# Two transformer blocks on one core: the last output projection by seven block products

## Chip, core and metric

One core of one Trainium2 chip. The metric is the device time of one execution in microseconds (us). Engines by their short names: PE is TensorE (PEld its weight loads), ACT ScalarE, DVE VectorE, POOL GpSimd, SP SyncE, whose queue issues every DMA of this kernel.

## The reference, cut to what matters

The last of three layers over T = 1024 tokens of width D = 1024 is banded attention with a gate:

```
q, z = split(h @ w_in, 2)                 # h: (1024, 1024)
out  = attention(q * HEAD_DIM**-0.5, k, v)  # 16 heads of 64, window 128, with sinks
y    = out * silu(z)                      # (1024, 1024)
h    = h + rms_norm_2(y @ w_out, post_g)  # the last projection, and the result
```

The layer before it has a projection of the same form, `y @ w_out` with y (1024, 2048). It is called the middle projection here. All arrays are fp32.

## The kernel before

Every large product is made from fp32 operands that are split in two fp32r parts, `hi` (an ACT copy) and `lo` (a DVE subtraction). `a @ b` becomes three matmuls: hi·hi, hi·lo, lo·hi. Weights come in pieces (`wraw`, 128x2x512 for projections), are split by `w_split_half` (L285 and L286: ACT makes `whi`, DVE makes `wlo`), and are fetched and split some pieces ahead, one half piece at a tick; a tick comes every four matmuls. At ticks the lanes advance too (generators that emit the work beside the matmuls), as do stores that were put off for some ticks and `jit`, which splits streamed activations. The program order on each engine is the order in which Python emits it, and each engine, SP's queue too, runs its own instructions in that order.

**Attention stage (`phase4`).** For each pair of heads p = 0 to 7 it computes q, the attention, and z. When a z half (512 tokens) is done, `make_z` takes its tanh on ACT and `gate_z` makes the gated output in two DVE operations (L2498, L2499); then ACT and DVE split it at once into `yb` hi and lo (L2501, L2503), which stay in SBUF: 16 halves of 128x512.

**Last projection (`run` in `out_proj`, L1884).** Two halves of 512 tokens (`half`), each by two halves of 512 output columns (`c`), each by four token tiles `j` of 128 and K = 8 slices of 128. That is 2 x 2 x 4 x 8 x 3 = 384 matmuls of 128x512. After each tile's last matmul ACT squares PSUM with a row sum (L1891) and DVE multiplies by the gain (L1892). For the first half `norm` finishes the tiles in a lane. For the second half the columns 512 to 1023 go tile by tile, and `last` finishes each tile: a sum, eleven more DVE operations on one column (an inverse square root by Newton steps, L456 to L470), two DVE operations of 128x512 that scale and add the residual (L1932), two stores.

**Middle projection (`run7`, L2044).** Its y and its weights are cut in four blocks each, and seven products of sums and differences of blocks replace eight. A product n = 0 to 6 is 512 tokens by 512 columns: four token tiles, each with its own PSUM bank. The weight differences (`TW`) were made by POOL during an earlier stage (`out_weights`) and kept in DRAM; the y blocks and their sums were stored to DRAM (`Y7`) and come back through `stream`, are split there by L1751 (ACT) and L1752 (DVE), about one product ahead of use. After the last matmuls of a product `evac` combines its PSUM tile with earlier products: an ACT copy (n = 0, 1), or a DVE sum (`plus`, L1998); finished output quarters go through `out`: an ACT square with row sum (L1993) and a multiplication by the gain (L1994, on POOL or DVE). After product 5, POOL adds the last quarter `c5` (L2015), and `last4` sends it through `out`.

`norm(0)` is the first token half's finish. It is emitted after product 4, beside product 5.

## Time and profile before

| what | value |
|---|---|
| median of 3 runs | 2471.33 us (2465.6 to 2472.78) |
| profiled execution | 2464.92 us, span 2463.1 us, granted PE clock 0.991 |
| busy in the span | PE 2407.2 us (98%), DVE 1451.9 (59%), ACT 1033.3 (42%), POOL 793.4 (32%) |

The times in rows count from the span's start. Matmuls are pipelined: a 128x512 matmul has a row of 389 ns while one follows the other every 227 ns (48 in 10.88 us). An engine's idle time stands in brackets behind the instruction that ended it, with what released it.

### The profile page before, as it was taken

What the parts mean: (1) busy time and instruction counts of PE and PEld (TensorE: products, weight loads), DVE (VectorE), ACT (ScalarE), POOL (GpSimd) and SP (SyncE); (2) the same over time, 40 slices, a digit from 0 to 9 for tenths busy, and PEclk for the clock granted to TensorE, in tenths of its full rate; (3) what the DMA queues carried; (4) which work ended last, traced back from release to release, by engine and by line L of the source; (5) the groups of instructions that cost most, each with busy time, mean ns of one, the idle gap of its engine ahead of it and who ended that gap; (6) DMA issues with size and microseconds to landing.
All of it is one profiled execution on the core that took longest, in us unless ns stands there. A gap on an engine that the chain in (4) does not pass through costs nothing.

```text
span 2463.1 us, 40015 instructions
## 1 busy us (share of the span) xinstructions
PE 2407.2 (98%) x14891; PEld 1899.8 (77%) x14891; DVE 1451.9 (59%) x3295; ACT 1033.3 (42%) x2539; POOL 793.4 (32%) x1023
## 2 busy tenths in 40 slices
PE   8999999999999999999999999999999998999998
PEld 6888777777777777777788777888878876777777
DVE  6765345545454345566747438656667587566545
ACT  4443222323232255664235223544545454566642
POOL 3443054433535032422420044545553033300000
PEclk8999999999999999999999999999999999999999
DMA  4334321111213355665834223334336842200033
GB/s 141 105 108 131 70 74 40 57 48 42 58 44 82 98 165 194 221 204 166 267 135 165 90 80 104 106 116 123 93 111 234 312 154 66 75 27 27 27 127 130
DMA packets 286262, 284.22 MB, mean 115 GB/s; under 512 B 27787, under 2 KB 208075, under 8 KB 286068
## 3 DMA queue, kind: packets, MB, share of 16 engines
q1 hardware_dynamic: 286068, 281.67, 36.6%
q8 instruction: 117, 1.92, 0.3%
q14 instruction: 77, 0.63, 0.1%
HBM read 206.87 MB, written 74.74 MB: 114 GB/s over the span
## 4 chain that ended last, share of the span: by engine, by line
PE 84%; DVE 6%; DMA 4%; ACT 3%; issue 2%; SPq 0%; POOL 0%; DVEq 0%; ACTq 0%; POOLq 0%
PE pd L349 39%; PE pd L391 8%; PE psP L391 8%; PE pb L2044 4%; PE pb L1884 4%; PE pd L1884 3%; PE psO L1157 2%; PE pb L1056 2%; PE pb L1122 2%; DMA vg<-Vd 1%; PE pb L349 1%; PE pd L2044 1%; DVE wlo L286 1%; PE pb L2338 1%; PE pb L743 1%
## 5 line engine op out<-in xcount | busy, mean ns | idle before, releaser
L349 PE MATMUL pd<-Ahi,wlo 128*128 128x512 f32 x1232 | 497.0, 403 | 5.0 <-DVE wlo L286 5.0
L349 PE MATMUL pd<-Ahi,whi 128*128 128x512 f32 x1232 | 496.6, 403 | 3.7 <-ACT Ahi L502 2.3
L349 PE MATMUL pd<-Alo,whi 128*128 128x512 f32 x1232 | 496.3, 403 | 1.7 <-DVE Alo L503 1.7
L286 DVE TENSOR_TENSOR wlo<-wraw,whi 128x512 fp32r<-128x512 f32 x348 | 278.7, 832 | 143.2 <-ACT whi L285 142.5
L349 PEld LDWEIGHTS pd<-Ahi,whi 128*128 128x128 f32 x1232 | 233.7, 190 | 56.5 <-ACT Ahi L502 3.1
L349 PEld LDWEIGHTS pd<-Alo,whi 128*128 128x128 f32 x1232 | 233.7, 190 | 55.5 <-issue 4.6
L349 PEld LDWEIGHTS pd<-Ahi,wlo 128*128 128x128 f32 x1232 | 233.6, 190 | 55.0 <-DVE wlo L286 6.8
L285 ACT ACTIVATE whi<-wraw 128x512 fp32r<-128x512 f32 x348 | 200.9, 622 | 36.0 <-DMA wraw<-in_b_w_out_dram 12.5
L1752 DVE TENSOR_TENSOR wlo<-wraw,whi 128x512 fp32r<-128x512 f32 x144 | 120.7, 849 | 81.3 <-ACT whi L1751 81.3
L1086 ACT ACTIVATE P<-P,ST 128x192 f32<-128x192 f32 (+2 forms) x320 | 130.6, 410 | 59.1 <-DVE ST L1074 53.1
L1751 ACT ACTIVATE whi<-wraw 128x512 fp32r<-128x512 f32 x144 | 89.5, 623 | 96.5 <-POOL wraw L228 93.8
L349 PE MATMUL pd<-wlo,Ahi 128*128 128x512 f32 x256 | 101.4, 396 | 4.5 <-DVE wlo L286 4.4
L799 POOL TENSOR_TENSOR X<-UC,X 128x60 f32<-128x60 f32 (+24 forms) x248 | 78.6, 317 | 82.4 <-DVE UC L792 64.0
L228 POOL TENSOR_TENSOR wraw<-wraw 128x512 f32<-128x512 f32 x48 | 71.6, 1492 | 98.6 <-DVE wlo L1752 86.0
L349 PE MATMUL pd<-whi,Ahi 128*128 128x512 f32 x256 | 100.8, 394 | 0.1
L349 PE MATMUL pd<-whi,Alo 128*128 128x512 f32 x256 | 100.7, 393 | 0.0
L801 POOL TENSOR_TENSOR X<-X 128x60 f32<-128x60 f32 (+24 forms) x248 | 80.6, 325 | 19.4
L278 POOL TENSOR_TENSOR wraw<-wraw,bpg 128x512 f32<-128x512 f32 x32 | 35.9, 1151 | 148.0 <-DMA wraw<-in_b_w_in_dram 127.0
L1157 PEld LDWEIGHTS psO<-PT,V 128*64 128x64 f32 x1040 | 55.5, 137 | 34.0 <-issue 16.6
L1157 PE MATMUL psO<-PT,V 128*64 128x128 f32 x1040 | 75.8, 283 | 4.8 <-DVE PT L1137 3.4
L1599 ACT ACTIVATE far<-pd 128x512 f32<-128x512 f32 x36 | 33.1, 918 | 101.9 <-PE pd L349 87.2
L2318 ACT ACTIVATE vg<-vg,lnv 128x128 f32<-128x128 f32 x128 | 53.4, 483 | 42.6 <-DMA vg<-Vd 42.1
(448 smaller groups left out, 5494.4 us busy)
## 6 DMA issues: line engine op xcount, KB each, us to landing
wraw<-in_w_in_dram SPq DMA_DIRECT2D x82, 512.0 KB
wraw<-in_a_w_in_dram SPq DMA_DIRECT2D x48, 512.0 KB
yraw<-Y SPq DMA_DIRECT2D x28, 512.0 KB
QD<-far SPq DMA_DIRECT2D x36, 256.0 KB
tw<-in_a_w_out_dram SPq DMA_DIRECT2D x32, 256.0 KB
TW<-tw SPq DMA_DIRECT2D x32, 256.0 KB
gate<-GT SPq DMA_DIRECT2D x32, 256.0 KB
wraw<-in_w_out_dram SPq DMA_DIRECT2D x16, 512.0 KB
```

What stands on the lines that cost most here:

```text
L285: nc.scalar.activation(out=his[j], in_=t[:, s], func=AF.Copy)
L286: nc.vector.tensor_tensor(out=los[j], in0=t[:, s], in1=his[j].bitcast(F32), op=ALU.subtract)
L349: nc.tensor.matmul(ps, lhsT=a, rhs=b, start=(n == 0), stop=(n == last))
L391: nc.tensor.matmul(ps, lhsT=a, rhs=b, start=(n == 0), stop=(n == 11))
L799: nc.gpsimd.tensor_tensor(out=tv, in0=U[:, j:j + 1, 0:j].to_broadcast([128, w, j]), in1=X[:, b0:8, j:j + 1].to_broadcast([128, w, j]), op= ...
L801: nc.gpsimd.tensor_tensor(out=X[:, b0:8, 0:j], in0=X[:, b0:8, 0:j], in1=tv, op=ALU.add)
L1086: nc.scalar.activation(out=it["P"][j][:, c], in_=Sx[j][:, c], func=AF.Exp, scale=-1.0, bias=ST[:, 0, n:n + 1], accum_out=ST[:, 1, n:n + 1])
L1157: nc.tensor.matmul(O(h).rearrange("p (s x) -> p s x", s=2), lhsT=V[:, b - 1 + t, c:c + 64], rhs=rhs, start=t == tiles[0], stop=t == 1)
L1751: nc.scalar.activation(out=hi, in_=src, func=AF.Copy)
L1752: nc.vector.tensor_tensor(out=lo, in0=src, in1=hi.bitcast(F32), op=ALU.subtract)
L1884: nc.tensor.matmul(ps[j], lhsT=a, rhs=b, start=(k == 0 and n == 0), stop=(k == KT - 1 and n == 2))
L2044: nc.tensor.matmul(ps[j], lhsT=a, rhs=b, start=(k == 0 and m == 0), stop=(k == 7 and m == 2))
```

## The change

The last projection goes the way of the middle one: seven products with K = 4 slices each, 7 x 4 x 4 x 3 = 336 matmuls.

- The weight differences `TB` are made by `out_weights`, now with a name, target and K as arguments: 16 loads, 16 POOL subtractions and 16 stores of 128x512, in a lane of the attention stage.
- `gate_z` no longer splits. It stores the blocks of y (12 of the 16 halves) and makes 16 sums or differences on DVE (`ysum`), which it stores as well: 28 stores of 128x512 to `YB7`.
- `stream` loads `YB7` again (14 loads of 512 KB) and splits it during the projection: 28 ACT copies and 28 DVE subtractions. The first two loads are issued ahead of the last z half.
- The order of the products is `ids` = 0, 3, 1, 2, 4, 5, 6. Product 3 needs a block of y and no sum, so it is second. In this order the POOL sum `u` follows product 2, and product 3's tiles go straight to `out`.
- The last product goes tile by tile, with `evac` and `last` behind each tile. `last4` is emitted at once behind product 5. The two sets of residual tiles are loaded one product earlier.

The weights of the last projection are 14 pieces (16 before, since each token half fetched them anew).

```diff
+        self.YB7 = [dt(f"YB7_{n}", [4, 128, 512]) for n in range(7)]
+        self.TB = [dt(f"TB{n}", [4, 128, 512]) for n in range(4)]
...
+        self.ids = {"a_out": (0, 1, 2, 3, 4, 5, 6), "b_out": (0, 3, 1, 2, 4, 5, 6)}
...
+        def blocks(name, key, T, K, ids):
+
+            self.first[key] = len(pc)
+            v = km(I[name][0])
+            t = [x.rearrange("k p f -> p k f") for x in T]
+            b = (v[:, 0:K, 0:512], t[0], t[1], v[:, K:2 * K, 0:512], v[:, K:2 * K, 512:1024], t[2], t[3])
+            for i in ids:
+                for k in range(0, K, 2):
+                    pc.append((b[i][:, k:k + 2, :], "k", None))
+
+        blocks("a_w_out_2", "a_out", self.TW, 8, self.ids["a_out"])
...
-        for half in range(2):
-            proj("b_w_out_2", 8, half, "b_out", "k4")
+        blocks("b_w_out_2", "b_out", self.TB, 4, self.ids["b_out"])
...
             def evac(n, j, ps):
                 if n < 2:
                     t = (c1, c5)[n][j] = self.s2("og")
                     nc.scalar.copy(out=t, in_=ps)
                 elif n == 2:
                     c2[j] = plus(ps, c1[j], self.s2("og"))
+                    if ids[1] == 3:
+
+                        u[j] = c1[j]
+                        nc.gpsimd.tensor_tensor(out=u[j], in0=c2[j], in1=c5[j], op=add)
+                elif n == 3 and ids[1] == 3:
+                    out(0, 0, j, plus(ps, c1[j], self.s2("og")), nc.gpsimd)
                 elif n == 3:
                     out(0, 0, j, plus(ps, c1[j], c1[j]), nc.gpsimd)
                     u[j] = self.s2("og")
@@ -2013,16 +2029,30 @@
                 elif n == 5:
                     plus(ps, c2[j], c2[j])
                     nc.gpsimd.tensor_tensor(out=c5[j], in0=c2[j], in1=c5[j], op=add)
-                    if j == 3:
+                    if j == 3 and nxt is not None:
                         self.lane_n.add(last4())
+                    elif j == 3:
+                        for _ in last4(0):
+                            pass
                 else:
                     out(0, 1, j, plus(ps, c2[j], c2[j]), nc.vector)

-            def last4():
-                yield 6
+            def last4(wait=6):
+                yield wait
                 for j in range(4):
                     out(1, 1, j, c5[j], nc.gpsimd)
                     yield 1
...
-                self.jit_limit = 4 * n + 8 if n else 6
-                if n in (4, 6):
-                    load_x(n // 6)
-                for kp in range(4):
-                    w = self.w_get(i0 + 4 * n + kp)
+                self.jit_limit = KP * n + 2 * KP if n else 2 * KP - 2 * (ids[1] == 1)
+                if n == 4 - (nxt is None):
+                    load_x(0)
+                if n == 6 - (nxt is None):
+                    load_x(1)
+                if nxt is None and n == 6:
+
+                    self.drain(self.lane_n)
                     for j in range(4):
-                        for k in (2 * kp, 2 * kp + 1):
...
-                    self.w_free(i0 + 4 * n + kp)
+                        for kp in range(KP):
+                            part(n, kp, j, ps[j])
+                            if j == 3:
+                                self.w_free(i0 + KP * n + kp)
+                        evac(ids[n], j, ps[j])
+                        last(4 + j, [og[1][h, j] for h in range(2)], x[1][j], ss[1][:, :, j:j + 1])
+                    self.jit = None
+                    return
+                for kp in range(KP):
+                    for j in range(4):
+                        part(n, kp, j, ps[j])
+                        if kp == KP - 1:
+                            evac(ids[n], j, ps[j])
+                    self.w_free(i0 + KP * n + kp)
...
-        return run7 if name == "a_out" else run
+        return run7 if name in self.ids else run
...
-        lane_z = Lane(1)
-        self.lanes.append(lane_z)
+        lane_z, lane_t = Lane(1), Lane(2)
+        self.lanes += [lane_z, lane_t]
+        lane_t.add(self.out_weights("b_w_out_2", self.TB, 4))
...
                 s = slice(512 * half, 512 * half + 512)
-                t = self.s2("tz")
+                if p < 4:
+
+                    if half == 0:
+                        yb[p] = self.s4("yb")
+                    t = yb[p][:, s]
+                else:
+                    t = self.s2("tz")
+                ys[p, half] = t
                 nc.scalar.activation(out=t, in_=ps, func=AF.Tanh, scale=0.5)
-                if p < 1:
-                    yb[p, half] = self.s2("yb_hi", F32R), self.s2("yb_lo", F32R)
-                else:
-                    y = self.s4("yb", F32R)
-                    yb[p, half] = y[:, 0:512], y[:, 512:1024]
-                lane_z.add(gate_z(ps, t, self.Oh[p][:, s], *yb[p, half]))
...
+        def gate_z(p, half, ps, t, o):

             yield 1
             nc.vector.scalar_tensor_tensor(out=t, in0=t, scalar=1.0, in1=ps, op0=ALU.add, op1=ALU.mult)
             nc.vector.scalar_tensor_tensor(out=t, in0=t, scalar=0.5, in1=o, op0=ALU.mult, op1=ALU.mult)
-            yield 2
-            nc.scalar.activation(out=h, in_=t, func=AF.Copy)
+            pos = self.ids["b_out"].index
+            n = {(0, 0): 0, (1, 0): 3, (1, 1): 6}.get((p // 4, half))
+            if n is not None:
+                self.store(self.YB7[pos(n)][p % 4], t, 6)
             yield 1
-            nc.vector.tensor_tensor(out=l, in0=t, in1=h.bitcast(F32), op=ALU.subtract)
+            if half == 0:
+                return
+
+            def do(x, y, op, n):
+                t = self.s2("ysum")
+                nc.vector.tensor_tensor(out=t, in0=x, in1=y, op=op)
+                self.store(self.YB7[pos(n)][p % 4], t, 6)
+                return t
+            if p < 4:
+                do(ys[p, 0], ys[p, 1], ALU.subtract, 5)
+                yield 1
+                return
+            s1 = do(ys[p - 4, 1], ys[p, 1], ALU.add, 1)
+            yield 1
+            s2 = do(s1, ys[p - 4, 0], ALU.subtract, 2)
+            yield 1
+            do(ys[p, 0], s2, ALU.subtract, 4)
             yield 1

         for n, c in enumerate(self.order_b):
@@ -2508,6 +2567,13 @@
             i = self.first["bq"] + n if n < 2 else self.first["bqz"] + n - 2
             q = qs[n] if n < 2 else self.s4("q") if c < 8 else None
             for half in range(n < 2, 2):
+                if c == 15 and half:
+
+                    self.drain(lane_t)
+                    self.flush()
+                    actB = self.stream(self.YB7, 4, 4, 2)
+                    self.out3 = self.out_proj("b_out", 4, "b_post_g_2", self.X2, self.out, None, actB)
+                    self.jit_limit = 2
...
-        self.out3 = self.out_proj("b_out", 8, "b_post_g_2", self.X2, self.out, None, lambda k, half: yb[k, half])
-        for half in range(2):
-            self.out3(half, [self.lane_n])
+        self.out3([self.lane_n], Lane())
```

Where the change moves instructions, on DVE first, at the end of the program. Before: from the first token half's finish (the eight xr rows) over the second half's first columns to the first tile of the tail (og is the output tile, row the gain, lst and ms the first steps of the inverse square root; each of the four tiles has a multiplication, twelve such steps and two xr rows).

```order
L1946 SCALAR_TENSOR_TENSOR xr<-og,or,xr 128x512 x8
L286 TENSOR_TENSOR wlo<-wraw,whi 128x512 x10
L1892 TENSOR_TENSOR og<-pb,row 128x512 x2
L1892 TENSOR_TENSOR og<-pd,row 128x512 x2
L1892 TENSOR_TENSOR og<-pb,row 128x512
L1928 TENSOR_TENSOR lst<-oss 128x1
L470 TENSOR_SCALAR ms<-lst 128x1
```

After, from the first token half's finish (the eight xr rows) over product 5's sums (og<-pb,og) to the first tile of the last product:

```order
L1954 SCALAR_TENSOR_TENSOR xr<-og,or,xr 128x512 x4
L1760 TENSOR_TENSOR y_lo<-yraw,y_hi 128x512 x2
L1954 SCALAR_TENSOR_TENSOR xr<-og,or,xr 128x512 x4
L286 TENSOR_TENSOR wlo<-wraw,whi 128x512
L2006 TENSOR_TENSOR og<-pb,og 128x512
L286 TENSOR_TENSOR wlo<-wraw,whi 128x512
L2006 TENSOR_TENSOR og<-pb,og 128x512 x2
L2006 TENSOR_TENSOR og<-pd,og 128x512
L2006 TENSOR_TENSOR og<-pb,og 128x512
L2002 TENSOR_TENSOR og<-og,row 128x512
L1936 TENSOR_TENSOR lst<-oss 128x1
```

The split of the last weight piece (the two L286 rows), which stood far ahead of the tail before, now stands behind the first half's finish and among product 5's sums; and each tile of the tail has a sum of its own (L2006) ahead of its multiplication.

On ACT, the end of the program after the change (the L2001 rows are squares with row sums; in brackets stand the engines or DMA semaphores that a row waits for):

```order
L1759 ACTIVATE y_hi<-yraw 128x512 [waits DMAHW7_49]
L1759 ACTIVATE y_hi<-yraw 128x512
L285 ACTIVATE whi<-wraw 128x512 [waits DMAHW1_49,Activation_49]
L285 ACTIVATE whi<-wraw 128x512 [waits PE_49]
L2001 ACTIVATE junk,oss<-og 128x512 [waits PE_49,Pool_49] x3
L2001 ACTIVATE junk,oss<-og 128x512 [waits Pool_49]
L2001 ACTIVATE junk,oss<-og 128x512 [waits DVE_49] x4
```

Before, the squares there waited for PE alone or for DVE and PE; now four squares of the last quarter, which wait for POOL's additions, stand ahead of the squares of the last product's four tiles.

On SP's queue, around the start of the projection, after the change (tz and ysum are blocks and sums of y):

```order
L163 DMA YB_4_102<-ysum 128x512
L2111 DMA yraw<-YB_0_98 128x2x512 x2
L1427 DMA row<-in_b_post_g_dram 128x1024
L163 DMA YB_1_99<-tz 128x512
L163 DMA YB_6_104<-tz 128x512
L163 DMA YB_2_100<-ysum 128x512
L163 DMA YB_3_101<-ysum 128x512
L163 DMA YB_4_102<-ysum 128x512
L2111 DMA yraw<-YB_1_99 128x2x512 x2
```

Before, the weight loads stood there without a break (only the load of row between them); now the first product's two loads stand behind the stores of the seventh head pair, and the second product's behind those of the eighth.

## Rows read from the trace of the kernel before

**Rows 1.** The page: the span, and the chain that ended last by engine.
```profile
span 2463.1 us, 40015 instructions
...
PE 84%; DVE 6%; DMA 4%; ACT 3%; issue 2%; SPq 0%; POOL 0%; DVEq 0%; ACTq 0%; POOLq 0%
```

**Rows 2.** Busy time in one stretch of the last projection (span, then each engine).
```profile
2375.00:2400.00 25.00, 25.00 (x112) 20.67 (x112) 7.58 (x12) 6.92 (x16) 0.00 (x0) 1.00 0.47 168
```

**Rows 3.** The chain that ended last, in order of time: start, duration, what.
```profile
2433.01 10.88 PE pb L1884 x48
...
2458.50 0.75 DVE xr L1932
```

**Rows 4.** Timeline of PE where the last projection begins: start, duration, instruction.
```profile
2367.34 0.39 PE L349 MATMUL pd<-Ahi,wlo 128*128 128x512 f32 x1
2367.56 0.39 PE L1884 MATMUL pb<-whi,yb_hi 128*128 128x512 f32 x1
```

**Rows 5.** Timeline of all engines at the end: the last token tile.
```profile
2454.86 0.60 ACT L1891 ACTIVATE junk<-pd 128x512 f32<-128x512 f32 x1 [4.81 <-PE pd L1884]
...
2455.58 0.69 DVE L1892 TENSOR_TENSOR og<-pd,row 128x512 f32<-128x512 f32 x1 [1.17 <-ACT junk L1891]
2456.19 0.15 DVE L1928 TENSOR_TENSOR lst<-oss 128x1 f32<-128x1 f32 x1
...
2458.50 1.42 DVE L1932 SCALAR_TENSOR_TENSOR xr<-og,nt_y,xr 128x512 f32<-128x512 f32 x2
```

**Rows 6.** Timeline of DVE in the middle projection, from its fifth product's sums on.
```profile
1985.44 0.69 DVE L1998 TENSOR_TENSOR og<-pb,og 128x512 f32<-128x512 f32 x1 [0.95 <-PE pb L2044]
...
1994.50 0.69 DVE L286 TENSOR_TENSOR wlo<-wraw,whi 128x512 fp32r<-128x512 f32 x1
...
1996.91 0.16 DVE L1939 TENSOR_TENSOR ost<-oss 128x4 f32<-128x4 f32 x1
...
1999.28 2.74 DVE L1946 SCALAR_TENSOR_TENSOR xr<-og,or,xr 128x512 f32<-128x512 f32 x4
...
2005.96 0.69 DVE L286 TENSOR_TENSOR wlo<-wraw,whi 128x512 fp32r<-128x512 f32 x1
```

**Rows 7.** Timeline of POOL in the middle projection, at its last two products.
```profile
2017.31 6.28 POOL L2015 TENSOR_TENSOR og<-og 128x512 f32<-128x512 f32 x4 [39.39 <-DVE og L1998]
2023.55 3.27 POOL L1994 TENSOR_TENSOR og<-og,row 128x512 f32<-128x512 f32 x2
2026.99 2.99 POOL L1994 TENSOR_TENSOR og<-og,row 128x512 f32<-128x512 f32 x2 [0.17 <-ACT junk L1993]
```

**Rows 8.** Timeline of DVE in the middle projection's last product: one token tile.
```profile
2041.71 0.68 DVE L1998 TENSOR_TENSOR og<-pb,og 128x512 f32<-128x512 f32 x1
2043.17 1.46 DVE L1994 TENSOR_TENSOR og<-og,row 128x512 f32<-128x512 f32 x1 [0.79 <-ACT junk L1993]
```

**Rows 9.** Timeline of POOL in an earlier stage, one of ten operations in succession.
```profile
1510.75 1.30 POOL L2157 TENSOR_TENSOR sc<-sc,Ahi 128x512 f32<-128x512 f32 x1
```

**Rows 10.** Timeline of DVE in the same stretch: one-column steps of a square root.
```profile
1510.92 1.15 DVE L462 SCALAR_TENSOR_TENSOR nt_b<-nt_a,lv 128x1 f32<-128x1 f32 x1
1512.10 0.16 DVE L464 SCALAR_TENSOR_TENSOR nt_y<-nt_b,nt_y 128x1 f32<-128x1 f32 x1
```

**Rows 11.** Timeline of SP's queue: two loads of stored activations, behind stores.
```profile
1890.15 0.92 SPq L2075 DMA_DIRECT2D yraw<-Y  x2
```

**Rows 12.** Timeline of ACT: the splits of those two loads.
```profile
1893.97 1.15 ACT L1751 ACTIVATE y_hi<-yraw 128x512 fp32r<-128x512 f32 x2 [5.95 <-DMA yraw<-Y]
...
1895.81 1.15 ACT L1751 ACTIVATE y_hi<-yraw 128x512 fp32r<-128x512 f32 x2 [0.17 <-DMA yraw<-Y]
```

**Rows 13.** Timeline of DVE: a gate of the seventh head pair, second token half.
```profile
2358.16 0.68 DVE L2498 SCALAR_TENSOR_TENSOR tz<-tz,pd 128x512 f32<-128x512 f32 x1
2358.87 0.69 DVE L2499 SCALAR_TENSOR_TENSOR tz<-tz,Og 128x512 f32<-128x512 f32 x1
```

**Rows 14.** Timeline of POOL in the attention stage: idle time ahead in brackets.
```profile
2143.84 2.49 POOL L278 TENSOR_TENSOR wraw<-wraw,bpg 128x512 f32<-128x512 f32 x2 [27.29 <-DMA wraw<-in_b_w_in_dram]
```

More of the change, by code (lines that the diff above doesn't have):

```diff
@@ L1198, in att_tw @@
     def att_tw(self):
-        self.lane_t.add(self.out_weights())
+        self.lane_t.add(self.out_weights("a_w_out_2", self.TW, 8))
         yield 1
@@ L1395, in plan @@
         fm("a_zu", a_in, [c for ct in self.order_z for c in (4096 + 128 * ct, 128 * ct)], kind="s")
-        self.first["a_out"] = len(pc)
-        v = km(I["a_w_out_2"][0])
-        T_ = lambda n: self.TW[n].rearrange("k p f -> p k f")
-        for b in (v[:, 0:8, 0:512], T_(0), T_(1), v[:, 8:16, 0:512], v[:, 8:16, 512:1024], T_(2), T_(3)):
-            for k in range(0, 8, 2):
-                pc.append((b[:, k:k + 2, :], "k", None))
+        def blocks(name, key, T, K, ids):
[7 more added lines that the diff above has]
+        blocks("a_w_out_2", "a_out", self.TW, 8, self.ids["a_out"])
         self.order_b = [0, 1] + [c for p in range(2, 8) for c in (p, 6 + p)] + [14, 15]
@@ L1631, in att_load, with out_weights @@
         yield 1
-    def out_weights(self):
+    def out_weights(self, name, T, K):
         nc = self.nc
-        W = self.I["a_w_out_2"][0]
+        W = self.I[name][0]
         def load(r, c, k):
             t = self.s2("tw")
-            nc.sync.dma_start(t, W[1024 * r + 128 * k:1024 * r + 128 * k + 128, 512 * c:512 * c + 512])
+            x = 128 * (K * r + k)
+            nc.sync.dma_start(t, W[x:x + 128, 512 * c:512 * c + 512])
             return t
@@ L1645, in minus @@
             if n is not None:
-                self.store(self.TW[n][k], to, 7)
-        for k in range(8):
+                self.store(T[n][k], to, 7)
+        for k in range(K):
             b11, b12, b22 = load(0, 0, k), load(0, 1, k), load(1, 1, k)
@@ L1999, in plus @@
                 return to
+            ids = self.ids[name]
             def evac(n, j, ps):
@@ L2025, in last4, with part @@
                     yield 1
+            def part(n, kp, j, ps):
+                w = self.w_get(i0 + KP * n + kp)
+                for k in (2 * kp, 2 * kp + 1):
+                    ah, al = [t[:, 128 * j:128 * j + 128] for t in act(k, n)]
+                    wh, wl = w(k % 2)
+                    for m, (a, b) in enumerate(((ah, wh), (ah, wl), (al, wh))):
+                        nc.tensor.matmul(ps, lhsT=a, rhs=b, start=(k == 0 and m == 0), stop=(k == KT - 1 and m == 2))
+                        self.mms += 1
+                        if self.mms % 4 == 0:
+                            self.tick()
             i0 = self.first[name]
@@ L2033, in run7 @@
                     self.lanes = lanes
-                self.jit_limit = 4 * n + 8 if n else 6
-                if n in (4, 6):
-                    load_x(n // 6)
-                for kp in range(4):
-                    w = self.w_get(i0 + 4 * n + kp)
-                    for j in range(4):
-                        for k in (2 * kp, 2 * kp + 1):
-                            ah, al = [t[:, 128 * j:128 * j + 128] for t in act(k, n)]
-                            wh, wl = w(k % 2)
-                            for m, (a, b) in enumerate(((ah, wh), (ah, wl), (al, wh))):
-                                nc.tensor.matmul(ps[j], lhsT=a, rhs=b, start=(k == 0 and m == 0), stop=(k == 7 and m == 2))
-                                self.mms += 1
-                                if self.mms % 4 == 0:
-                                    self.tick()
-                        if kp == 3:
-                            evac(n, j, ps[j])
-                    self.w_free(i0 + 4 * n + kp)
+                self.jit_limit = KP * n + 2 * KP if n else 2 * KP - 2 * (ids[1] == 1)
[5 more added lines that the diff above has]
+                    self.drain(self.lane_n)
+                    for j in range(4):
+                        for kp in range(KP):
[12 more added lines that the diff above has]
+                    self.w_free(i0 + KP * n + kp)
                 if n == 4:
```

3 lines of the change are left out of this document (2 added, 1 removed).

## The prediction

> **What bounds the kernel now.** I began with the page: the chain that ended last lies on PE for 84% of the span [rows 1], so matmuls count where nothing else is late. Then the stage. The last projection starts 2367.56 us into the span, 0.22 us after the last z matmul [rows 4], and its last 96 matmuls are two pieces of the chain of waits of 10.88 and 10.89 us without a gap between them [rows 3]: 227 ns for one. The 384 matmuls take 87.1 us, to 2454.8. Inside, PE is busy for 25.00 of 25 us and DVE for 7.58 [rows 2]. So PE bounds this stage, with engines beside it that have room. After the last matmul comes a tail of 8.3 us on the last token tile: square, multiplication, the inverse square root on one column, scaling, store [rows 5]. The chain's last piece of an engine is there [rows 3]; the last scaling ends at 2459.9 and the span 3.2 us later [rows 1, 5].
>
> **What the change removes.** 384 less 336 is 48 matmuls, or one product of 10.9 us. If the tail stayed at 8.3 us, the span would shrink by that.
>
> **What it adds in the attention stage.** The 16 POOL subtractions (1.6 us each by the four additions of [rows 7], 26 us in all) find POOL idle: it sits idle for 27.3 us ahead of one weight gain there [rows 14], and goes on with such gaps. I price them at 0; without that cover, the weights of z would wait for at most those 26 us, less what is fetched ahead. On DVE 16 sums replace 16 lo subtractions of the same shape, on ACT 16 copies go. The stores go out on SP, whose queue holds weight loads there; these are fetched two pieces ahead, so 0 again, with 3 us either way for the range.
>
> **The start.** The first product's loads stand behind four stores of pair 7, the last of which needs a third sum of 0.7 us after the gate that ends at 2359.6 [rows 13]. So stores and loads are issued at about 2362. Two such loads behind stores were issued at 1890.15, and their splits began 3.8 and 5.7 us later [rows 11, 12]. That makes 2365.8 and 2367.7 here, and with 0.6 us on ACT and 0.7 on DVE the first slice is ready just before 2367.6; the second piece is needed 5.4 us later. But the tanh of the last z half now stands behind that second piece's two copies, some 1.3 us later than before, then come two gates, three sums and five stores, and only then the second product's loads: issued at 2373.4, usable at 2377.2, split by 2378.5, when PE asks for them at 2378.4. I take 1 us for the start, 0 and 5 as its bounds.
>
> **The steady products.** 28 splits of y and 28 of weights, 0.6 us each when they follow one another [rows 6], and the sums of `evac` now recur every 10.9 us instead of every 21.8. Up to product 3 DVE has four sums and eight splits in a product, 7.3 us, so it keeps up. From product 4 on it doesn't. There, its order is row for row that of the middle projection: four times sum and multiplication with a wait for ACT's square between them, splits, twelve steps of the root, eight xr rows with two splits among them, a weight split. In the trace that block runs from 1985.44 to 2006.65 [rows 6], 21.2 us with DVE waiting only for those squares. The middle projection had 21.8 us of matmuls in a product to hide it; this one has 10.9.
>
> Now the sum, in the old trace's time. Product 4 starts at 2367.6 + 1.0 + 4 x 10.88 = 2412.1; its first tile is complete 30 matmuls (6.8 us) and 0.1 us later [rows 3, 5], at 2419.0. DVE's block ends 21.2 us on, at 2440.2. Product 6 could start at 2433.9 but needs, 1.4 us in, the weight half that the block's last row splits. PE waits here, and it no longer matters, since DVE sets the end:
> - Product 5's first sum: 2440.8. Only now can POOL start `c5`: four additions, 6.3 us [rows 7], to 2447.1.
> - ACT has all four squares of `c5` ahead of that of the tail's first tile. Two squares of 0.8 us [rows 5]: 2448.7.
> - The first tile's multiplication, steps and scaling: 2.9 us from multiplication to scaling and 1.4 for the two xr rows [rows 5], 4.3 in all. POOL meanwhile multiplies `c5` by the gain until about 2453.5 (6.4 us for four [rows 7]). In [rows 9, 10] a one-column DVE step beside a POOL operation takes 1.15 us in place of 0.16 and every second one is held; a multiplication takes 1.46 for 0.69 [rows 5, 8]. The tile's first DVE rows meet three POOL operations; I take 4.0 us for that, 0 and 5 as bounds. First tile done: 2457.0.
> - Three tiles more. DVE waits in each for the square between sum and multiplication, 1.46 us from the one to the other [rows 8], then 4.3: 5.8 us a tile, against 2.7 us of PE. Done at 2474.4.
> - The last store, 3.2 us: 2477.6.
>
> **The span grows by 14.5 us.** The profiled execution took 2464.92 us, so 2479.4, or +0.59%. It lies 0.26% under the median of the runs shown, 2471.33; scaled to that, 2485.8 us. I take 2485.5.
>
> The Trainium skill, page "SBUF — State Buffer", section "Who interferes with whom", says that a VectorE instruction with two SBUF inputs and a GpSimd instruction that reads SBUF share a port under an exclusive lock, and that the loser waits for the other's whole instruction. It speaks against putting eight POOL operations beside this tail. By the page alone, the multiplication and the two steps behind it with two SBUF inputs would each wait out a POOL operation of 1.6 us at most, 4.8 us, and the sum would be 15.3; by the rows it is 14.5. The trace agrees in kind: sums with one input from PSUM kept their 0.68 us beside POOL, the two-input multiplication did not [rows 8].
>
> **Rivals.**
> - *The tail is serial but nothing is late into it* (DVE catches up before product 6, say because splits are done earlier than the order lets me believe). Then product 6's first tile is complete at 2436.7, four tiles of 5.8 us end at 2459.9 and the span at 2463.1: no change. For it: DVE waits a lot ahead of product 4. Against it: the block is in order behind product 4's first sum.
> - *Late, but POOL does not hold the tail.* From 2440.2 five rows of 0.6 us, four tiles: 2466.4, and the span is 2469.6, +6.5 us or 0.26%, within what can be told.
> - *Faster:* the tail's tiles hide beside each other as before, and the whole product is gained: 2367.6 + 1 + 76.2 + 8.3 = 2453.1, -10.0 us. It decides if a tile costs DVE no more than the 2.7 us in which PE makes one. In the trace a tile took 4.3 us of DVE without the sum [rows 5]; hidden then because PE needed 5.4 for one.
> - *The round trip stalls PE at the start too:* both first products wait, 5 us in place of 1, and the contention is at its bound: +20 us.
>
> **Chances.** Forecast with its variants down to +8 us and up to +13 for other sizes of hold and lock: 0.64. Start worse: 0.12. Late without hold: 0.09. Nothing late: 0.10. Faster: 0.05. About 0.3% (7.4 us) can be told from no change: the first two give slower 0.76, the next two 0.19 for the same, 0.05 faster. Without the last two cases the range is +3 to +22 us on 2471.3: 2474 to 2493, which leaves out some 0.17 with the runs' own scatter.
>
> **What would show it.** Right: 336 matmuls in the last projection; product 4's first sum some 51 us after its start; a gap of several us on PE just inside product 6; POOL's four additions behind a late sum of product 5; four DVE tiles of 5.8 us, the first longer; the tail from last matmul to end over 20 us. Wrong: DVE idle ahead of product 6, ACT's last four squares not held behind POOL, or the tail tiles at PE's pace. A gap at the first or second product longer than 2 us would put the loss at the round trip, and new waits of PE among the z groups at the attention stage.

## The result, and the profile after

The median of 7 runs is 2484.97 us (2480.68 to 2492.2), beside 2472.78 us (2464.73 to 2475.87) for the kernel before. The ratio of the runs is 1.0068, with a 95% interval of 1.0054 to 1.0081: slower by about 17 us if the ratio is applied to the time before, and inside the range forecast. The two medians as such lie 12.2 us apart. The profiled execution's span is 2482.8 us, 19.7 more than [rows 1].

Three marks cut those 19.7 us: the first long group of attention products (`psO`, at 2152.83 us before and 2155.61 after), the first matmul of the last projection, and the end. Up to `psO` it is 2.8 us; in the ten profiled executions whose program is the same, or nearly, up to there, that mark lies between 2148.1 and 2158.9, so this is scatter. From `psO` to the projection it is 220.56 us in place of 214.73. From the projection's start to the end it is 106.63 in place of 95.54. The kernel before has one profile, so its two stretches are those of one execution.

**The projection.** PE after the change, around the start and in the last product: start, duration, instruction, in brackets the idle time and what ended it.

```profile
2375.94 0.39 PE L349 MATMUL pd<-Ahi,wlo 128*128 128x512 f32 x1
2376.17 0.39 PE L2052 MATMUL pb<-whi,y_hi 128*128 128x512 f32 x1
...
2447.88 0.80 PE L2052 MATMUL pb<-wlo,y_hi 128*128 128x512 f32 x1 [4.66 <-DVE wlo L286]
```

The first product does not wait for its round trip through DRAM: it starts 0.23 us after the last z matmul, as in [rows 4]. The only wait inside the projection is for the weight split that the forecast named. In the 6 us behind it (2448 to 2454 us) the granted clock is 0.50, the lower of the two levels (1.2 GHz), and a 128x512 matmul follows the other every 427 ns; no row of DVE waits for PE there, so this costs nothing. DVE, from product 4's first sum to the tail's second tile, and the last scaling:

```profile
2426.78 0.69 DVE L2006 TENSOR_TENSOR og<-pb,og 128x512 f32<-128x512 f32 x1 [0.75 <-PE pb L2052]
...
2440.63 2.74 DVE L1954 SCALAR_TENSOR_TENSOR xr<-og,or,xr 128x512 f32<-128x512 f32 x4
...
2447.14 0.69 DVE L286 TENSOR_TENSOR wlo<-wraw,whi 128x512 fp32r<-128x512 f32 x1
2447.74 0.69 DVE L2006 TENSOR_TENSOR og<-pb,og 128x512 f32<-128x512 f32 x1
...
2455.29 1.65 DVE L2002 TENSOR_TENSOR og<-og,row 128x512 f32<-128x512 f32 x1 [3.87 <-ACT junk L2001]
2456.86 1.24 DVE L1936 TENSOR_TENSOR lst<-oss 128x1 f32<-128x1 f32 x1
...
2458.51 0.84 DVE L460 TENSOR_TENSOR nt_a<-nt 128x1 f32<-128x1 f32 x1
...
2462.28 0.68 DVE L2006 TENSOR_TENSOR og<-pb,og 128x512 f32<-128x512 f32 x1
2463.75 0.69 DVE L2002 TENSOR_TENSOR og<-og,row 128x512 f32<-128x512 f32 x1 [0.79 <-ACT junk L2001]
...
2478.11 1.41 DVE L1940 SCALAR_TENSOR_TENSOR xr<-og,nt_y,xr 128x512 f32<-128x512 f32 x2
```

The block that is 21.2 us long in [rows 6] is 21.0 us here, and it ends some 6 us behind product 5's last matmul (six products of 10.88 us from the start: 2441.5). POOL and ACT behind it, the additions of `c5`, its gain, and the squares:

```profile
2448.56 5.33 POOL L2031 TENSOR_TENSOR og<-og 128x512 f32<-128x512 f32 x4 [26.09 <-issue]
2453.85 5.49 POOL L2002 TENSOR_TENSOR og<-og,row 128x512 f32<-128x512 f32 x4
```
```profile
2450.20 0.63 ACT L2001 ACTIVATE junk<-og 128x512 f32<-128x512 f32 x1 [10.82 <-POOL og L2031]
...
2453.92 0.63 ACT L2001 ACTIVATE junk<-og 128x512 f32<-128x512 f32 x1 [0.52 <-POOL og L2031]
...
2454.55 0.62 ACT L2001 ACTIVATE junk<-og 128x512 f32<-128x512 f32 x1
```

ACT's square of the tail's first tile (2454.55) follows the last of `c5`, and DVE sits idle for 3.87 us before its multiplication. Then the other three tiles follow one another at 5.72 us (2462.28, 2468.00, 2473.72), where PE has made the last of them by 2460.3.

**The attention stage.** Before the change one group of DVE's scalings of P took 1.01 us, and PE waited 0.34 us:

```profile
2169.25 1.01 DVE L1106 TENSOR_SCALAR P<-P,rd 128x192 f32<-128x192 f32 x4
```
```profile
2169.71 1.04 PE L1122 MATMUL pb<-K,P 128*128 128x128 f32 x6 [0.34 <-DVE P L1106]
```

After the change the same four rows, POOL beside them, and PE:

```profile
2171.04 1.23 DVE L1100 TENSOR_TENSOR es<-es,ST 128x4 f32<-128x4 f32 x1
...
2172.52 3.67 DVE L1106 TENSOR_SCALAR P<-P,rd 128x192 f32<-128x192 f32 x4
```
```profile
2170.48 4.58 POOL L1652 TENSOR_TENSOR tw<-tw 128x512 f32<-128x512 f32 x3 [0.55 <-DMA tw<-in_b_w_out_dram]
2175.03 4.95 POOL L278 TENSOR_TENSOR wraw<-wraw,bpg 128x512 f32<-128x512 f32 x4
```
```profile
2173.86 0.58 PE L1122 MATMUL pb<-K,P 128*128 128x128 f32 x3 [1.70 <-DVE P L1106]
2175.23 0.33 PE L1122 MATMUL pb<-K,P 128*128 128x128 f32 x1 [0.80 <-DVE P L1106]
2176.25 0.44 PE L1122 MATMUL pb<-K,P 128*128 128x128 f32 x2 [0.68 <-DVE P L1106]
...
2355.97 1.51 PE L1122 MATMUL pb<-K,P 128*128 128x128 f32 x6 [4.11 <-DVE P L1106]
```

One by one the four scalings take 1.19, 0.31, 1.32 and 1.09 us, and each of the three long ones ends some 0.1 us behind the end of a POOL row; the last of these POOL rows is a weight gain, not a difference. The last row of PE is a second place: that wait was 2.98 us before, and two of the new sums stand ahead of the score maxima there.

```profile
2349.72 1.03 PE L1122 MATMUL pb<-K,P 128*128 128x128 f32 x6 [2.98 <-DVE P L1106]
```

From `psO` to the projection all of PE's waits but one of 0.5 us end with DVE's P: 8.35 us after the change, 5.24 before. None ends with a DMA, so the new stores and loads hold nothing there directly. The difference, 3.1 us, is the waits' part of the 5.8. The other 2.7 stand in no wait of PE; the granted clock behind the last wait can make up to 3.0 of them (an estimate: 6 us at 0.50 in place of 1.00). Behind that wait the granted clock falls. After, and before, with the clock in the third column from the right:

```profile
2356.00:2362.00 6.00, 6.00 (x26) 4.78 (x28) 4.26 (x13) 1.68 (x6) 0.00 (x0) 0.51 0.13 46
```
```profile
2350.00:2356.00 6.00, 6.00 (x43) 4.68 (x42) 4.62 (x13) 3.98 (x14) 0.00 (x0) 1.00 0.01 3
```

### The profile page after: what moved, and what is told of

Same layout as the page of the kernel before. It is cut to its first block, busy times and chain, and to the rows that moved or that the text cites. A ratio compares the mean times of both kernels' runs of the same rounds, so it can differ in the third digit from the quotient of the medians.

```text
span 2482.8 us, 40226 instructions
## 1 busy us (share of the span) xinstructions
PE 2403.1 (97%) x14843; PEld 1896.5 (76%) x14843; DVE 1486.6 (60%) x3331; ACT 1042.4 (42%) x2555; POOL 832.4 (34%) x1055
## 4 chain that ended last, share of the span: by engine, by line
PE 81%; DVE 8%; DMA 4%; ACT 3%; issue 2%; POOL 1%; SPq 0%; DVEq 0%; ACTq 0%; POOLq 0%
PE pd L349 39%; PE pd L391 8%; PE psP L391 7%; PE pb L2052 5%; PE psO L1157 3%; DMA vg<-Vd 2%; PE pb L1122 2%; PE pb L1056 2%; PE pb L1892 2%; PE pd L1892 2%; PE pd L2052 2%; DVE wlo L286 1%; PE pb L2374 1%; PE pb L349 1%; ACT vg L2354 1%
## 5 line engine op out<-in xcount | busy, mean ns | idle before, releaser
L286 DVE TENSOR_TENSOR wlo<-wraw,whi 128x512 fp32r<-128x512 f32 x344 | 273.1, 821 | 143.5 <-ACT whi L285 139.3
L285 ACT ACTIVATE whi<-wraw 128x512 fp32r<-128x512 f32 x344 | 199.9, 622 | 27.0 <-PE pd L2052 13.5
L1760 DVE TENSOR_TENSOR wlo<-wraw,whi 128x512 fp32r<-128x512 f32 x144 | 120.8, 849 | 81.3 <-ACT whi L1759 81.3
L1759 ACT ACTIVATE whi<-wraw 128x512 fp32r<-128x512 f32 x144 | 89.4, 623 | 95.9 <-POOL wraw L228 93.2
L2052 PE MATMUL pb<-wlo,y_hi 128*128 128x512 f32 x252 | 100.3, 398 | 5.2 <-DVE wlo L286 5.2
L2052 PE MATMUL pb<-whi,y_hi 128*128 128x512 f32 x252 | 100.2, 398 | 1.6 <-ACT whi L285 1.6
L2052 PE MATMUL pb<-whi,y_lo 128*128 128x512 f32 x252 | 99.8, 396 | 0.0
L1652 POOL TENSOR_TENSOR tw<-tw 128x512 f32<-128x512 f32 x48 | 63.9, 1331 | 67.9 <-DMA tw<-in_b_w_out_dram 35.0
```

The source lines that it names most:

```text
L285: nc.scalar.activation(out=his[j], in_=t[:, s], func=AF.Copy)
L286: nc.vector.tensor_tensor(out=los[j], in0=t[:, s], in1=his[j].bitcast(F32), op=ALU.subtract)
L1759: nc.scalar.activation(out=hi, in_=src, func=AF.Copy)
L1760: nc.vector.tensor_tensor(out=lo, in0=src, in1=hi.bitcast(F32), op=ALU.subtract)
L2052: nc.tensor.matmul(ps, lhsT=a, rhs=b, start=(k == 0 and m == 0), stop=(k == KT - 1 and m == 2))
```

## The experiments

Times in the table are from each profile: from `psO` to the projection's start, from there to the end; the ratio to the kernel before is from the timed runs.

| run | psO to projection | projection to end | ratio (95%) |
|---|---|---|---|
| before | 214.7 | 95.5 | |
| after | 220.6 | 106.6 | 1.0068 (1.0054 to 1.0081) |
| e0_after_again | 220.6 | 107.0 | 1.0080 (1.0067 to 1.0093) |
| e1_gain_pool | 220.6 | 106.2 | 1.0067 (1.0055 to 1.0079) |
| e2_norm_behind | 220.8 | 108.2 | 1.0078 (1.0065 to 1.0090) |
| e3_one_root | 220.7 | 99.4 | 1.0046 (1.0033 to 1.0059) |
| e4_tb_early | 216.0 | 106.7 | 1.0114 (1.0101 to 1.0127) |
| e5_sums_late | 221.4 | 107.1 | 1.0060 (1.0046 to 1.0074) |
| e6_y_ahead | 221.1 | 106.4 | 1.0065 (1.0053 to 1.0077) |
| e7_no_finish | 220.5 | 99.6 | 1.0047 (1.0035 to 1.0059) |
| e8_no_gain | 220.6 | 104.3 | 1.0066 (1.0053 to 1.0079) |
| e9_tb_mid | 215.6 | 106.6 | 1.0040 (1.0026 to 1.0054) |
| best2 | 215.7 | 95.9 | 1.0043 (1.0030 to 1.0056) |
| best3 | 215.6 | 91.7 | 0.9980 (0.9971 to 0.9989) |

The intervals reach some 3 us to either side. By them e3, e7, e9, best2 and best3 are faster than e0 and e4 is slower; the smaller differences below rest on the stretches, each of one profile.

My theory was the forecast's: DVE falls behind from product 4 on. Its rivals were a tail that is simply serial, and a loss in the attention stage.

**e0_after_again**, the changed kernel once more. 

> The changed kernel itself, a second time, to tell scatter from cost. Theory (DVE falls behind from product 4 on, and its late rows push product 5's sums, c5, ACT's squares and the four serial tiles of the tail): from the first matmul of the last projection to the end of the span 106.6 us again, within 1 us, with PE's wait of 4 to 5 us inside product 6 again. Rival (the loss lies in the attention stage: POOL's differences, stores, the clock): the start of the projection stands about 8.6 us later than in the kernel before again. If that start moves by several us from the first profile, part of the 8.6 is scatter. The time about 2485, within 4.

The projection starts 11.2 us later than before in this execution, in place of 8.6, but the 2.6 us more lie ahead of `psO`. Both stretches repeat within 0.4 us, so each is a cost of the program and not scatter; the rival is right in that the attention stage pays 5.8 us each time.

**e1_gain_pool**

```diff
-                    out(1, 0, j, plus(ps, u[j], u[j]), nc.vector)
+                    out(1, 0, j, plus(ps, u[j], u[j]), nc.vector if nxt is not None else nc.gpsimd)
```

> Product 4's four multiplications by the gain go from DVE to POOL, so DVE loses four multiplications and its waits for ACT's squares between sum and multiplication. Theory: the weight split that PE waits for in product 6 ends about 4 us earlier, PE's wait there shrinks from 4.7 to about 0.6 us, product 5's first sum and all behind it come 4 us earlier, and from the projection's first matmul to the end it is 102.6 us in place of 106.6. Rival (the four serial tiles set the tail whatever DVE did before): no change from 106.6, at most 1 us.

Missed: 0.4 to 0.8 us in place of 4. That is the rival's number, but not a test of it, since the block hardly shrank (20.4 us for 21.0). DVE in the same stretch shows where the room went:

```profile
2426.12 1.36 DVE L286 TENSOR_TENSOR wlo<-wraw,whi 128x512 fp32r<-128x512 f32 x1 [1.31 <-ACT whi L285]
...
2430.68 1.39 DVE L286 TENSOR_TENSOR wlo<-wraw,whi 128x512 fp32r<-128x512 f32 x1 [1.40 <-ACT whi L285]
2431.99 2.39 DVE L1760 TENSOR_TENSOR y_lo<-yraw,y_hi 128x512 fp32r<-128x512 f32 x2
```

Four splits take 5.14 us in place of 2.7 beside POOL's multiplications, and DVE now waits twice for a weight copy that stands on ACT behind a square of DVE's own sum. Most of the work moved from DVE to POOL was charged to DVE again.

**e2_norm_behind**

```diff
-                if n == 4:
+                if n == (4 if nxt is not None else 5):
                     self.lane_n.add(norm(0, og[0], x[0], ss[0], 18, 2, 26))
```

> The first token half's finish (root and eight xr rows) is emitted behind product 5 in place of product 4, so behind product 5's sums and ahead of the tail's tiles; DVE's work is the same. Theory: no wait of PE in product 6, POOL's c5 additions start at about 64.6 us after the projection's start in place of 72.4, the eight rows fill the idle time that DVE had before the tail's first multiplication, and projection's start to end falls to 101 to 103 us. Rival (only what stands among the tail counts): the finish now stands ahead of the tail with 8 us, and the time rises by 6 to 8 us, to 113 to 115.

PE's wait is gone, and `c5` starts 64.95 us after the projection's start, as expected. The sum came out between the two theories, since the root now stands beside POOL:

```profile
2441.45 1.22 DVE L470 TENSOR_SCALAR ms<-ost 128x4 f32<-128x4 f32 x1
2442.71 1.21 DVE L456 TENSOR_SCALAR nt<-ms 128x4 int32<-128x4 int32 x1
2443.96 1.21 DVE L460 TENSOR_TENSOR nt_a<-nt 128x4 f32<-128x4 f32 x1
```

Six such rows in succession take 1.21 or 1.22 us, and the twelve steps together 9.2 us in place of 2.4. I had not priced that.

**e3_one_root**

```diff
-                        last(4 + j, [og[1][h, j] for h in range(2)], x[1][j], ss[1][:, :, j:j + 1])
+                    for _ in norm(1, og[1], x[1], ss[1]):
+                        pass
+                    self.flush()
```

> The four tiles of the last product are finished together: four times sum, square and multiplication, then one inverse square root for four columns and eight xr rows, in place of four roots in turn. Theory: DVE's chain from the first multiplication of the tail (1.7) goes on with three tiles of 2.1 us, a root of 2.4 and eight rows of 5.5 us; that is 8 us less than the four serial tiles, so 98 to 99 us from the projection's start to the end. Rival (DVE's lateness alone is the loss, the tail is as short as PE allows): no change or some us slower, since now no tile is done until the last one is.

99.4 us, just above the 98 to 99 expected and 7.6 less than e0: the four roots in turn are that dear once DVE sets the end. Finishing tile by tile pays only while DVE keeps up with PE.

**e4_tb_early**

```diff
         self.lane_t.add(self.out_weights("a_w_out_2", self.TW, 8))
+        self.lane_t.add(self.out_weights("b_w_out_2", self.TB, 4))
...
-        lane_t.add(self.out_weights("b_w_out_2", self.TB, 4))
```

> POOL's 16 differences of the last projection's weights are made right behind those of the middle one, in an earlier stage, and not beside this attention. Theory (in the attention stage POOL's two-operand rows hold DVE's scaling of P, 3.67 us in place of 1.01 for four rows, and PE waits behind them): the three waits of 1.7, 0.8 and 0.7 us at one place become one of 0.3, and from the first long group of attention products (psO, 2152.8 us in the kernel before) to the last projection's first matmul it is 217.9 us, in place of 220.7 with the change and 214.7 before. Rival (stores and loads on SP and in the DMA queues delay the stage): no change from 220.7. Where the differences now stand, at most 1 us is added. Time -2 to -3 us against the changed kernel.

At the old place the three waits are gone (none above 0.4 us stands there), and the stretch is 216.0, shorter than I thought. At the new place I missed: at most 1 us was expected, and `psO` comes at 2171.7. In the first layer's attention PE waits 19.0 us between 1070 and 1200 us, in place of 7.6 in e0: 11.8 for DVE's copies into `PT`, 5.8 for its score maxima, 1.4 for a copy on ACT. POOL clears `PT` behind the differences there; that these late clears hold the copies is likely, not shown:

```profile
1095.85 1.65 POOL L1653 TENSOR_TENSOR tw<-tw 128x512 f32<-128x512 f32 x1 [8.15 <-PE pd L349]
1097.43 0.34 POOL L1125 MEMSET PT<- 64x128 f32 x2
1097.74 3.14 POOL L1653 TENSOR_TENSOR tw<-tw 128x512 f32<-128x512 f32 x2
1100.83 0.34 POOL L1125 MEMSET PT<- 64x128 f32 x2
```

**e5_sums_late**

```diff
+            if p == 5:
+                yield 4
             s1 = do(ys[p - 4, 1], ys[p, 1], ALU.add, 1)
```

> The three sums of the sixth head pair are emitted four ticks later, so that they stand behind the score maxima and the next scaling of P on DVE, not ahead of them. Theory (two sums of 0.6 us ahead of the maxima make PE's wait 4.1 in place of 3.0 us, and behind that wait the granted clock stands at 0.5 for some 6 us): the wait falls to 2.7 to 3.0 us, the granted clock behind it stays at 1.00, and from that group psO to the projection's first matmul it is 217.2 us in place of 220.7. Rival (the wait is that for ACT's copies, whatever DVE does first, or the clock falls by itself): wait and clock as they were, 220.7.

Inconclusive. At its place the wait is 2.92 us and the clock behind it stays at 1.00, as the theory said. But the whole stretch is no shorter: at the other place, where the edit changes no order, P took 4.23 us in place of 3.67 in this execution, PE waited 4.4 us in place of 3.2, and the granted clock was 0.71 there. The later runs speak against my reading: without the differences, the stretch is the same with the sums early (e9) and late (best3).

**e6_y_ahead**

```diff
-                self.jit_limit = KP * n + 2 * KP if n else 2 * KP - 2 * (ids[1] == 1)
+                self.jit_limit = KP * n + (2 if nxt is not None else 3) * KP if n else 2 * KP - 2 * (ids[1] == 1)
```

> The splits of y run one product further ahead: so two pairs of y splits (2.4 us) leave DVE's block behind product 4's first sum. DVE's work is the same, POOL's too. Theory: PE's wait in product 6 falls from 4.65 to about 2.2 us, and all that follows, c5 and the tail, comes 2.4 us earlier: 104.4 us from the projection's start to the end in place of 106.8. Rival (the tail does not hang on DVE's block): 106.8 within 0.5.

Missed: 0.2 to 0.6 us in place of 2.4, the rival's number once more. The block shrank by 2.4 us and PE's wait in product 6 to 2.25, as expected; but the earlier y splits stand ahead of a weight split, PE waits 1.08 us for that at an earlier product, and product 4's first sum stands 52.5 us after the start in place of 50.6. The block ends 71.2 us after the projection's start in place of 71.7, and the end moves by as little. So the end still follows the block's end, not its length.

**e7_no_finish**

```diff
+                    if nxt is None:
+                        for j in range(4):
+                            self.store(xdst[128 * j:128 * j + 128, :], x[0][j], 6)
...
-                if n == 4:
+                if n == 4 and nxt is not None:
                     self.lane_n.add(norm(0, og[0], x[0], ss[0], 18, 2, 26))
```

> Leaves out the first token half's finish in the last projection: its inverse root (twelve steps) and its eight xr rows on DVE; these 512 tokens are stored without the projection's part. Theory: DVE loses about 8 us of its block behind product 4, so PE's wait of 4.65 us in product 6 is gone, c5's additions start about 65 us after the projection's start (72.4 with the finish), the tail's first multiplication follows the last addition, and from the projection's start to the end it is 96 to 98 us in place of 106.8. Rival (DVE's block is not what makes the tail late): 105 us or more.

7.5 us less than e0, PE's wait gone, `c5` from 64.94 us on (the projection starts at 2379.43):

```profile
2444.37 5.37 POOL L2031 TENSOR_TENSOR og<-og 128x512 f32<-128x512 f32 x4 [18.42 <-issue]
```

It is the plainest evidence for the late block. It ends 1.6 us above what I expected: I had left out the hold of the first tile by POOL, which is still there (2.7 us, next).

**e8_no_gain**

```diff
                 nc.scalar.activation(out=jk, in_=t, func=AF.Square, accum_out=ss[half][:, c, j:j + 1])
-                eng.tensor_tensor(out=t, in0=t, in1=gpost[:, 512 * c:512 * c + 512], op=ALU.mult)
+                if eng is not None:
+                    eng.tensor_tensor(out=t, in0=t, in1=gpost[:, 512 * c:512 * c + 512], op=ALU.mult)
...
-                    out(1, 1, j, c5[j], nc.gpsimd)
+                    out(1, 1, j, c5[j], nc.gpsimd if nxt is not None else None)
```

> Leaves out POOL's four multiplications of c5 by the gain, so the last quarter of the output lacks its gain. Nothing else is changed. Theory (POOL's two-operand rows hold DVE's rows in the tail's first tile: 1.65, 1.24 and 0.84 us for 0.69, 0.15 and 0.16): these three rows fall to 0.69, 0.15 and 0.16 us, and the projection takes 104.1 us in place of 106.8. Rival (these rows are long for a reason of their own, not for POOL): no change. The one additional possibility is that ACT's squares, not POOL, are late; then the multiplication starts at the same time but is short.

104.3 us, 2.7 less than e0 and 2.3 less than the first profile, and the three rows are short:

```profile
2452.26 0.69 DVE L2003 TENSOR_TENSOR og<-og,row 128x512 f32<-128x512 f32 x1 [3.90 <-ACT junk L2001]
2452.87 0.15 DVE L1936 TENSOR_TENSOR lst<-oss 128x1 f32<-128x1 f32 x1
...
2453.43 0.16 DVE L460 TENSOR_TENSOR nt_a<-nt 128x1 f32<-128x1 f32 x1
```

**e9_tb_mid**, the differences alone moved into the first layer's output projection.

```diff
+        lane_tb = Lane(1)
+        lane_tb.add(self.out_weights("b_w_out_2", self.TB, 4))
         for half in range(2):
-            run(half, [self.lane_n, self.lane_g])
+            run(half, [self.lane_n, self.lane_g, lane_tb])
+        self.drain(lane_tb)
...
-        lane_t.add(self.out_weights("b_w_out_2", self.TB, 4))
```

> The weight differences alone are moved, into the first layer's output projection, where POOL is nearly idle; all else as in the changed kernel. Theory (beside the attention the differences cost 4.7 us through DVE's rows and the waits of PE behind them, as the version with the differences in the earlier attention stage gave 216.0 us from the group psO to the projection's start; where PE runs long rows and DVE has room they cost nothing): 216 us from psO to the projection's start in place of 220.7, psO between 2150 and 2156, 106.8 us in the projection, and 4 to 5 us less than the changed kernel. Rival (the differences cost the same 5 us or more wherever they are): psO later than 2158, and no gain.

As expected: 215.6 us, `psO` at 2151.3. Nothing is lost where they stand now: PE is busy for 87.70 of 87.70 us of the first layer's output projection, with POOL busy for 25.01 us beside it (1246.7 to 1334.4 us). In the changed kernel it was the same with POOL busy for 1.67 us (1249.4 to 1337.1). In the attention stage the scalings are short again:

```profile
2167.27 1.01 DVE L1106 TENSOR_SCALAR P<-P,rd 128x192 f32<-128x192 f32 x4
```

So of the 5.8 us there 4.9 go with the differences, their loads and stores included, and 0.9 with all else (sums, stores of y, the absent lo splits). 3.2 of the 4.9 are the three waits; the rest is in no wait, and the clock behind the last wait, 0.77 here in place of 0.50, may be it (1.6 us by the same estimate).

**best2** has e4's, e5's and e6's edits, weight splits one piece further ahead, one root, `c5` added on DVE, the xr rows spread over products 5 and 6, and in `out` the multiplication kept for the next tile (`settle` runs the kept work first):

```diff
+                settle()
+                pend.append((t, gpost[:, 512 * c:512 * c + 512]))
```

> All that the theory names, undone together: differences early, sums of the sixth pair late, y splits one product and weight splits one piece further ahead, each multiplication by the gain behind the next tile's sum, c5 added on DVE, the first half's xr rows spread over products 5 and 6, one root for the last four tiles. Theory: no wait of PE inside the projection above 1 us, 89 to 92 us from its start to the end (95.5 in the kernel before), about 215 us from the group psO to its start, and so 3 to 6 us faster than before. Rival (DVE and POOL cannot carry products of 10.9 us however their rows are ordered): 99 us or more in the projection, slower than before.

The stretch to the projection came as expected; the projection did not: 95.9 us. DVE still waited up to 1.4 us at a time for weight copies behind squares on ACT, and two xr rows beside POOL took 3.48 us. And e4's place is dear again: `psO` comes at 2163.2.

**best3** keeps the square back as well, has e9's place for the differences, and the old limit for weight splits.

```diff
+                settle()
+                pend.append((c, half, j, t, eng))
```

> As the version with all edits, but the weight differences are made in the first layer's output projection, where POOL is idle for most of 100 us and DVE is used for 60%, and each square waits behind the next tile's sum as the multiplication does, so that ACT's weight copies no longer stand behind a square that waits for DVE. Theory: no wait of PE at the place of the three waits in the attention stage, about 215 us from the group psO to the projection's start, nothing lost where the differences now stand, 91 to 94 us from the projection's start to the end (95.5 before); span 2459 to 2463, so 1 to 4 us faster than before, which can hardly be told. Rival (POOL's 26 us cost DVE the same wherever they stand): the group psO starts 8 us or more later than the kernel before has it.

91.7 us in the projection, 215.6 before it, `psO` at 2150.55. The median of 12 runs is 2461.87 us (2458.8 to 2468.58) beside 2466.96 for the kernel before: the interval lies below 1 as a whole, so the seven products, with the work around them reordered, gain 0.1 to 0.3% on the kernel before, which was given none of these reorderings. DVE still ends the program: its last sum starts at 2444.54, where PE is done with the last tile by 2442.5.

```profile
2444.54 0.68 DVE L2023 TENSOR_TENSOR og<-pd,og 128x512 f32<-128x512 f32 x1
...
2448.99 5.39 DVE L1959 SCALAR_TENSOR_TENSOR xr<-og,or,xr 128x512 f32<-128x512 f32 x8
```

## Why the prediction was right, point by point

- **What is removed.** 48 matmuls are gone and the rest go at the pace forecast, but for the 6 us behind PE's wait. Without that wait and the lower clock behind it PE would have been done 76 us after its start; it was done after 84.2.
- **The attention stage** is the step that failed. It was priced at 0 because POOL is idle there, with 3 us either way. POOL was idle, as said; the cost fell on DVE. The stage lost 5.8 us or more in every execution with the differences there, and e9 gives 4.9 of them back: 3.2 as waits for DVE, the rest not assigned. The cover that I named (idle time of POOL) was the wrong engine's. The same hold was in my own sum, at the tail. The Trainium skill's page "SBUF — State Buffer", section "Who interferes with whom", names `tensor_scalar` too among the operations that can take the shared port, and three of the four rows at 2172.52 us agree; I had weighed its rule for two-input rows alone.
- **The start** was priced at 1 us, between 0 and 5: it is 0. Counted from the first matmul, the second product's loads were issued at 5.8 us and their first lo slice was ready at 11.1 (5.8 and 10.9 forecast). But the lo slice is first needed by that product's third matmul, at 11.3: it came in time by 0.2 us.
- **The steady products.** Product 4's first sum stands 50.6 us after the start (51 forecast); the block is 21.0 us (21.2), PE's wait in product 6 is 4.66 us. e7 shows that the block makes the tail late, by 7.5 us.
- **The tail.** `c5`'s additions took 5.3 us (6.3 forecast) and the hold of the first tile 2.7 (4.0, of 0 to 5), both from e8 and the rows above. By the rule of the Trainium skill's page "SBUF — State Buffer", section "Who interferes with whom", the forecast gave an estimate of 4.8 for that hold; the three rows lost 0.96, 1.09 and 0.68 us to it. Three tiles at 5.72 us (5.8). So the projection took 106.6 us where the sum said 109.0, and e3 shows that the serial roots are 7.6 us of it.
- **The number.** 14.5 us were forecast, 1 at the start and 13.5 in the projection. The runs show 5.8 before it and 11.1 to 11.5 in it, about 17, as the ratio says. Two errors of opposite sign, +4.8 ahead of the projection and some -2.2 in it, partly cancel: the size is better than its parts, and that the time forecast, 2485.5 us, lies 0.5 us from the median is luck. The rivals "nothing late" and "late without hold" are excluded, the one by PE's wait and e7, the other by e8; the round trip stalled nothing.

Against 84.6 us (95.5 less the product saved) the projection was 22 us too long. e7, e3 and e8 take 7.5, 7.6 and 2.7 us from the same chain, one at a time; such parts need not add up, and best3, which takes 15.3 together, shows no more than that most of it is the order of the work on DVE and of what waits for it. What stays open is the price of the sums ahead of the maxima: a wait of 4.07 us at that place in e9 and one of 2.87 in best3 both went with 215.6 us for the stretch, with the granted clock behind them at 0.77 and 0.50. That clock differs between executions of one program too (below), so the price can't be read from these two.

## What to carry to other kernels

Smaller products leave every other engine less time for each (10.9 us here, 21.8 in the middle projection), while the sums, gains and finish of a product stay as long: price the in-order block of the busiest helper against the new length, before pricing the matmuls. Idle time of POOL is no cover by itself. Look at what DVE does beside it, since here many of DVE's rows with SBUF inputs alone grew longer beside POOL's two-operand rows, and put POOL's rows where PE has long rows and DVE has slack, as e9 did. A finish tile by tile hides only while the finishing engine is faster than the one that it follows; once it isn't, finish the tiles together.

## What the runs showed of the hardware that was not expected

- Beside POOL's rows of 128x512, many DVE rows with SBUF inputs alone were stretched towards the length of a POOL row, however small: a 128x4 step 1.21 us for 0.16 (six in succession in e2), three of four scalings of 128x192 1.09 to 1.32 us for 0.31. Not all were: one of those scalings kept 0.31, a reciprocal of 128x4 its 0.18, two 128x1 steps of the tail their 0.15. In the earlier stage of [rows 10] mostly every second step was.
- After PE's wait at the end of the attention stage the granted clock is not the same from execution to execution, even where the program up to there is the same, and the wait's length doesn't tell which it is. In the 6 us from the end of the wait: 1.00 after 2.98 us (before) and 2.92 (e5), but 0.50 after 2.87 (best3); 0.77 after 4.07 (e9). After 4.11 to 4.13 us, with one program up to there, it was 0.50 or 0.51 in the changed kernel, e0, e1 and e7, and 0.72 to 0.75 in e2, e3, e6 and e8. 0.50 is the lower of the two levels, 1.2 GHz. The second four had a clock of 0.72 to 0.77 for some 6 us already at the three waits some 180 us earlier, where the first four had 1.00. Over the stretch as a whole this nearly evens out: 220.5 to 220.8 us in seven of the nine executions with the differences there, 221.1 (e6) and 221.4 (e5) in the other two. So a clock seen behind one wait in one profile is no price of that wait.
